# Stick-breaking scan with PSUM constants in two parts, products on POOL, a lag of four steps, and four more gate units by seven quarter products

## The chip, the cores and the metric

The kernel runs on one core of one Trainium2 chip. The metric is the device time of one execution in microseconds, the median of several runs of the same program on the same chip; lower is better. The engines are named as in the profile: PE (TensorE, matrix products; PEld is its weight load, which overlaps), DVE (VectorE), ACT (ScalarE), POOL (GpSimd) and SP (SyncE), whose queue issues nearly all DMAs.

## The reference, cut to what matters

One inference step of a hybrid encoder layer: 1024 prompt frames and 64 sample frames of 1024 channels, all in float32. Each frame is normalised and multiplied by a matrix of 1024 x 6144 columns, which gives query, key, value and gate of two attention branches with 8 heads of 64 channels each, and two branch gates of 1024 columns.

```python
# branch sb: stick breaking, s < t
z = einsum("bqhd,bkhd->bhqk", q, k) * 0.125
log_keep = where(causal, log_sigmoid(-z), 0.0)
suffix = cumsum(log_keep, axis=3, reverse=True) - log_keep
w = where(causal, exp(log_sigmoid(z) + suffix), 0.0)
o = einsum("bhqk,bkhd->bqhd", w, v)
# branch cb: softmax over the last 512 keys and the own chunk, with a clipped relative-position bias
# merge
b_sb = (o_sb * silu(z_sb)) @ w_proj_sb
b_cb = (o_cb * silu(z_cb)) @ w_proj_cb
h = sigmoid(g_sb) * b_sb + sigmoid(g_cb) * b_cb
y = x + h @ w_out
```

So a weight of branch sb is sigmoid(z) of its key times the product of sigmoid(-z) over all later keys below the query: the length of stick that is left.

## The kernel before, in words

Float32 matrices are split into a high part and a remainder, both in a format that PE multiplies at full rate, and a product is three passes (high by high, high by low, low by high). Stages, by the time in the profile:

- 0 to 227 us: normalisation, transposes, and the projections that are wanted with frames on partitions (values, queries and keys of cb).
- 227 to 483 us, line 634: twelve pairs of column units (list `pairs`: queries and keys of sb, both SiLU gates, the gate `g_sb`) by the seven-product scheme for two by two block matrices: sums of quarters of the weights are made on DVE, split on ACT and POOL, and instead of eight quarter products there are seven, each of two column pieces (256 and 288) with 4 x 3 passes. `emit` (line 563) brings the results through ACT and DVE to DRAM.
- The other eight units (list `units`, the gate `g_cb`) are plain products, line 782: each has three column groups (384, 384, 320) of 24 products. They come from a generator, `run_fill`, and are called in small numbers by `fill(n)` between the steps of the two attention stages, so that PE has work while other engines are at it; behind the units the generator goes on with the sb output projection (`proj_sb`, line 882). A group gathers in a bank of PSUM from the pool `psF`, which has two, and is copied out by ACT (`ev_act`).
- 483 to 507 us, the lead-in: six calls of `fill(24)` with the loads of the first sb pair of heads between them, all on SP: `load_k` of the sample (tile kss), `load_q` of the sample (sqs), `load_k` of the prompt (ks), `load_q` (sq), `load_v`, `load_z`.
- 507 to 680 us branch sb, 680 to 835 us branch cb. A list `seq` has, for each of four pairs of heads, the sample tile (t = 8, both heads at once) and then eight query tiles of 128 frames for either head: 17 steps. Steps of sb have 576 or (t + 1) x 128 keys, of cb 576 or up to 640.
- 835 to 985 us: projections of cb, merge and output projection.

What a step is made of, in the order of the program at iteration i: `qk(i)` has PE make the scores z (line 1033), and for sb ACT writes sigmoid(-z) into the tile kp (line 1036) and sigmoid(z) into be (line 1037), with POOL setting the one element of kp behind the last key. Then the loads for coming steps go to SP. `mid(i - 1)`, for sb, has DVE run a scan over kp from the last key to the first (line 1056): state = kp x state + constant, where the constant is a row of zeros with an identity matrix at its end (`imp`, in SBUF), which starts each row at its own query and so does the causal mask as well; then DVE multiplies be by the result (line 1057). Half of the fill follows, then `av` (line 1127: value products of a finished block of two query tiles and both heads, gated on DVE at line 1132 and stored), then `tr(i - LAG)`, which transposes the weights on PE (line 1088) into one of two PSUM tiles pt and copies them to SBUF (tile wT): for sb always on ACT (line 1097), for cb one time in four on ACT and else on DVE (line 1099). Then the other half of the fill. LAG is 3. For cb, `soft` (exponential on ACT, line 1047) and `mid` (reciprocal on DVE, scaling on ACT, line 1060) stand at the head of the iteration.

Each engine works through its own instructions in this order. Every engine's order is written out by hand; no scheduler moves anything. How many fill products an iteration gets is in proportion to its number of keys (for cb plus 150): 144 in the lead-in, 336 in sb, 288 in cb.

## Time and profile before

| | us |
|---|---|
| median of 3 runs (985.58 to 986.71) | 986.17 |
| the profiled execution | 986.78 |
| its span, first to last instruction | 985.0 |
| seven-product stage | 227 to 483 |
| lead-in | 483 to 507 |
| sb | 507 to 680 |
| cb | 680 to 835 |

The page gives the busy time of each engine and the chain of work that ended last; a busy table by stretches gives the same for each stage; the order in time of one engine shows when an instruction began and how long it took. Instructions of PE overlap, so the spacing of their starts, not their length, is what one costs. L with a number is a line of the kernel before. PE's granted clock is 1.0 throughout.

### The profile page before, as it was taken

What the parts mean: (1) busy time and instruction counts of PE and PEld (TensorE: products, weight loads), DVE (VectorE), ACT (ScalarE), POOL (GpSimd) and SP (SyncE); (2) the same over time, 40 slices, a digit from 0 to 9 for tenths busy, and PEclk for the clock granted to TensorE, in tenths of its full rate; (3) what the DMA queues carried; (4) which work ended last, traced back from release to release, by engine and by line L of the source; (5) the groups of instructions that cost most, each with busy time, mean ns of one, the idle gap of its engine ahead of it and who ended that gap; (6) DMA issues with size and microseconds to landing.
All of it is one profiled execution on the core that took longest, in us unless ns stands there. A gap on an engine that the chain in (4) does not pass through costs nothing.

```text
span 985.0 us, 20439 instructions
## 1 busy us (share of the span) xinstructions
PE 962.0 (98%) x7568; PEld 917.6 (93%) x7568; DVE 630.1 (64%) x1188; ACT 510.4 (52%) x1142; POOL 346.2 (35%) x356
## 2 busy tenths in 40 slices
PE   5999999999999999999999999999999999999998
PEld 5999999999999999999998888898888888999998
DVE  5456665696454655532239898997767765599735
ACT  5534443344443433433248787786876875466220
POOL 3376664115444554444211101101201101486641
PEclk9999999999999999999999999999999999999999
DMA  6727567533656333343298656666898772852642
GB/s 229 223 89 243 193 223 253 166 103 120 180 174 203 115 110 101 99 124 99 79 244 221 172 160 161 164 187 169 232 262 226 213 221 68 264 177 83 210 131 86
DMA packets 174243, 166.97 MB, mean 170 GB/s; under 512 B 34688, under 2 KB 160000, under 8 KB 174016
## 3 DMA queue, kind: packets, MB, share of 16 engines
q1 hardware_dynamic: 165424, 157.34, 53.7%
q10 hardware_dynamic: 8720, 8.33, 2.6%
q8 instruction: 60, 0.98, 0.4%
q14 instruction: 39, 0.32, 0.1%
HBM read 106.89 MB, written 58.72 MB: 168 GB/s over the span
## 4 chain that ended last, share of the span: by engine, by line
PE 90%; DMA 3%; ACT 3%; DVE 1%; SPq 1%; issue 1%; POOL 1%; DVEq 0%; ACTq 0%
PE b L634 25%; PE acc L464 19%; PE b L1435 8%; PE o L1127 7%; PE acc L782 7%; PE z L1033 6%; PE pt L1088 6%; PE b L924 5%; PE acc L882 3%; DMA wrawx<-in_w_in_dram 1%; PE pk L349 1%; ACT wT L1097 1%; PE pt L277 1%; SPq L51 1%; PE acc L1471 1%
## 5 line engine op out<-in xcount | busy, mean ns | idle before, releaser
L122 POOL TENSOR_TENSOR wlo<-wraw,whi 128x1024 fp32r<-128x1024 f32 x22 | 57.6, 2618 | 103.0 <-ACT whi L115 102.9
L1088 PE MATMUL pt<-ident,be 128*128 128x128 f32 (+1 forms) x568 | 87.2, 278 | 5.7 <-ACT wT L1097 1.9
L1056 DVE TENSOR_TENSOR_SCAN kp<-kp,imp 128x128 f32<-128x128 f32 (+7 forms) x64 | 88.3, 1379 | 0.6 <-ACT kp L1036 0.6
L1033 PE MATMUL z<-ks,sq 128*128 128x320 f32 (+5 forms) x384 | 83.2, 325 | 0.0
L1088 PEld LDWEIGHTS pt<-ident,be 128*128 128x128 f32 (+1 forms) x568 | 65.9, 140 | 16.8 <-issue 5.7
L1097 ACT ACTIVATE wT<-pt 128x512 f32<-128x512 f32 (+3 forms) x125 | 58.6, 501 | 39.0 <-PE pt L1088 38.9
L464 PE MATMUL acc<-whi,xa 128*128 128x256 f32 x256 | 74.2, 292 | 0.0
L464 PE MATMUL acc<-wlox,xm 128*128 128x256 f32 x256 | 70.8, 278 | 0.0
L464 PE MATMUL acc<-whi,xm 128*128 128x256 f32 x256 | 70.8, 278 | 0.0
L464 PE MATMUL acc<-wlo,xa 128*128 128x256 f32 x256 | 70.7, 278 | 0.0
L464 PE MATMUL acc<-whix,xb 128*128 128x256 f32 x256 | 70.7, 278 | 0.0
L464 PE MATMUL acc<-whix,xm 128*128 128x256 f32 x256 | 70.6, 278 | 0.0
L1033 PEld LDWEIGHTS z<-ks,sq 128*128 128x128 f32 x384 | 65.8, 188 | 1.1 <-issue 0.2
L1127 PE MATMUL o<-wT,vp 128*64 128x256 f32 (+1 forms) x608 | 66.7, 357 | 0.1
L782 PE MATMUL acc<-xm,whi 128*128 128x384 f32 (+1 forms) x192 | 65.2, 340 | 0.0
L1127 PEld LDWEIGHTS o<-wT,vp 128*64 128x64 f32 x608 | 42.3, 136 | 23.9 <-issue 5.7
L1057 DVE TENSOR_TENSOR be<-be,kp 128x128 f32<-128x128 f32 (+8 forms) x68 | 57.3, 843 | 9.4 <-ACT sg L757 0.5
L1036 ACT ACTIVATE kp<-z 128x384 f32<-128x384 f32 (+6 forms) x104 | 52.4, 504 | 9.5 <-PE z L1033 4.5
L642 DVE TENSOR_TENSOR u<-b,s 128x256 f32<-128x256 f32 (+1 forms) x48 | 20.8, 439 | 56.3 <-PE b L634 55.2
L1037 ACT ACTIVATE be<-z 128x384 f32<-128x384 f32 (+6 forms) x104 | 52.9, 508 | 0.0
L1060 ACT ACTIVATE be<-be,sm 128x640 f32<-128x640 f32 (+5 forms) x68 | 47.2, 694 | 9.5 <-DVE sm L1059 9.2
L1047 ACT ACTIVATE be<-be,sm 128x640 f32<-128x640 f32 (+5 forms) x68 | 47.2, 694 | 3.7 <-DVE sm L1039 3.4
(300 smaller groups left out, 3147.4 us busy)
## 6 DMA issues: line engine op xcount, KB each, us to landing
wraw<-in_w_in_dram SPq DMA_DIRECT2D x32, 512.0 KB, 4.6
wrawx<-in_w_in_dram SPq DMA_DIRECT2D x16, 512.0 KB, 4.5
sq<-d_qsbT SPq DMA_DIRECT2D x32, 192.0 KB, 3.6
sq<-d_qcbT SPq DMA_DIRECT2D x32, 192.0 KB, 4.4
xt<-in_x_prompt_dram SPq DMA_DIRECT2D x8, 512.0 KB, 5.8
d_kcbT<-hl SPq DMA_DIRECT2D x8, 512.0 KB, 4.4
d_qcbT<-hl SPq DMA_DIRECT2D x8, 512.0 KB, 5.7
d_ksbT<-hl SPq DMA_DIRECT2D x16, 256.0 KB, 2.5
```

Of the source, the lines that this page charges most:

```text
L122: (eng or G).tensor_tensor(out=l, in0=raw, in1=h[:].bitcast(F32), op=OP.subtract)
L464: TE.matmul(ps, x, w, start=m == 0, stop=m == len(steps) - 1)
L634: TE.matmul(ps[:, :m], w[:, hl_, k], right[s](x)[:, k, a:b], start=s < 3 and k == 0 and e == 0, stop=k == 3 and e == 2, skip_group_check=s ...
L782: TE.matmul(ps[:, :b - a], w[:, k], xk(x, k)[:, a:b], start=k == 0 and n == 0, stop=k == KT - 1 and n == 2)
L1033: TE.matmul(z[:, :m], s[:, e, q0:q0 + 128], ks[:, h, o + x:o + y], start=e == parts[0][0], stop=e == parts[-1][0])
L1037: A.activation(be[:r, x:y], z[:r, :m], AF.Sigmoid, scale=0.125)
L1056: V.tensor_tensor_scan(kp[:r, n - 1::-1], kp[:r, n - 1::-1], im[:, ::-1], 0.0, op0=OP.mult, op1=OP.add)
L1057: V.tensor_tensor(out=be[:r, :n], in0=be[:r, :n], in1=kp[:r, 1:n + 1], op=OP.mult)
L1088: TE.transpose(pt[:kr, x, :r], be[:r, kb * 128:kb * 128 + kr], ident[:r, :r])
L1097: A.activation(w[:, sl:sl + m, q0:q0 + r], pt[:, :m, :r], AF.Copy)
L1127: TE.matmul(o[hd * 64:hd * 64 + 64, c0:c1], vv[:kr, kb, hd * 64:hd * 64 + 64], wT[b, p, j, hd, s // 4][:kr, s % 4, c0:c1] if j < 4 else wT ...
L1435: TE.matmul(ps[:, t], left[s](xs_, k)[:, ts_], wt_[:, k], start=s < 3 and t == k == e == 0, stop=k == 3 and e == 2, skip_group_check=s > 2 ...
```

## The change

1. The lists: four of the eight plain units go to `pairs` as two more pairs (14 instead of 12), kind "copy".
2. The pool `psF` of two banks becomes two pools of one bank each, `psF` and `psG`, used in turn by `facc()`. During sb, `psG` holds the scan's constants (the identity, its half for the sample tile, and one zero), and fill has `psF` alone; `fill` then stops at the end of a group of 24, in the first half of an iteration one product ahead of it, and carries the rest over. In cb there are two banks again.
3. The scan is done in two parts: the last 128 keys (64 for the sample) with the identity as its constant, and the keys before them with the zero as the constant of all elements and the first part's result as its start value. The product goes from DVE to POOL.
4. LAG is 4, with one more buffer each for be and kp. In sb the copies of transposed weights alternate between ACT and DVE.
5. The lead-in has `fill(12)` six times. How much fill an iteration gets comes from a plan (`share`), which sets an estimate of PE's work in it against one of the other engines': 72 in the lead-in, 168 in sb, 228 in cb. The rest runs behind cb.
6. The last unit's first group is done in sb. Its second group, in cb, issues the loads of the sb outputs for `proj_sb`; fill is held from the end of the first group until the sixth iteration of cb.

```diff
-    units = [("ev_act", 5120 + 128 * j, (AF.Copy, d_g["cb"][j])) for j in range(KT)]
+    pairs += [("copy", 5120 + 128 * j, d_g["cb"][j:j + 2]) for j in range(0, 4, 2)]
+    units = [("ev_act", 5120 + 128 * j, (AF.Copy, d_g["cb"][j])) for j in range(4, KT)]
...
-    psF = ctx.enter_context(tc.tile_pool(name="af", bufs=2, space=PS))
+    psF = ctx.enter_context(tc.tile_pool(name="af", bufs=1, space=PS))
+    psG = ctx.enter_context(tc.tile_pool(name="ag", bufs=1, space=PS))
+    banks = [psF, psG]
+
+    def facc():
+        banks.append(banks.pop(0))
+        return banks[-1].tile([128, 512], F32, name="acc")
...
-                A.activation(sg[:, :n], src[:, :n], AF.Sigmoid)
+                A.activation(sg[:, :n], src[:, :n], AF.Copy if kind == "copy" else AF.Sigmoid)
...
-                        if ci == k == n == 0 and j + 1 == len(units):
+                        if ci == 1 and k == n == 0 and j + 1 == len(units):
                             load_og("sb", 0, late["y"])
...
-                            if ci == 2:
-                                prog[0] = j
+                            prog[0] = 3 * j + ci
...
-    def fill(n):
+    sent = [0]
+
+    def fill(n, part=2):
         n += owed[0]
         owed[0] = 0
+        room = 22 + part - sent[0] % 24 if len(banks) == 1 else n
         while n > 0:
-            if prog[0] == len(units) - 2 and "sb" not in late:
+            if room <= 0:
+                owed[0] = n
+                return
+            room -= 1
+            if prog[0] == 3 * len(units) - 3 and "sb" not in late:
...
-        be = am.tile([128, NP], F32, name="be", bufs=4)
+        be = am.tile([128, NP], F32, name="be", bufs=5)
...
-            kp = ax.tile([128, NP + 2], F32, name="kp", bufs=3)
+            kp = ax.tile([128, NP + 2], F32, name="kp", bufs=4)
...
-            im = ims[:] if t == 8 else imp[:, NP - n:NP]
-            V.tensor_tensor_scan(kp[:r, n - 1::-1], kp[:r, n - 1::-1], im[:, ::-1], 0.0, op0=OP.mult, op1=OP.add)
-            V.tensor_tensor(out=be[:r, :n], in0=be[:r, :n], in1=kp[:r, 1:n + 1], op=OP.mult)
+            m = n - (64 if t == 8 else 128)
+            imp = late["imp"]
+            last = kp[:, n - 1:m - 1 if m else None:-1]
+            V.tensor_tensor_scan(last, last, imp[:, 191:127:-1] if t == 8 else imp[:, 127::-1], 0.0,
+                                 op0=OP.mult, op1=OP.add)
+            if m:
+                V.tensor_tensor_scan(kp[:, m - 1::-1], kp[:, m - 1::-1], imp[:, 192:193].to_broadcast([128, m]),
+                                     kp[:, m:m + 1], op0=OP.mult, op1=OP.add)
+            G.tensor_tensor(out=be[:r, :n], in0=be[:r, :n], in1=kp[:r, 1:n + 1], op=OP.mult)
...
-                if b == "sb" or flip[0] % 4 == 0:
+                if flip[0] % (2 if b == "sb" else 4) == 0:
...
-        fill(24)
+        fill(12)
         flush()
         f()
+    imp = late["imp"] = psG.tile([128, 512], F32, name="acc")
+    V.tensor_copy(imp[:, 0:128], ident)
+    for h in (slice(0, 64), slice(64, 128)):
+        V.tensor_copy(imp[h, 128:192], ident[h, h])
+    V.memset(imp[:, 192:193], 0.0)
+    banks[:] = [psF]
...
-    LAG = 3
+    LAG = 4
...
+    def share(i):
+        b, p, t, hd = seq[i]
+        n = band(b, t)[1]
+        pe, v = (4 if t == 8 else 2) * n / 2.2, n * 1.45 + 900
+        if i >= LAG:
+            pe += 109 * ((band(*seq[i - LAG][::2])[1] + 127) // 128)
+        if i > LAG and closes(i - LAG - 1):
+            b2, _, t2, _ = seq[i - LAG - 1]
+            pe += sum(432 * (z - y) / 256 for _, y, z in av_steps(b2, t2 // 2 if t2 < 8 else 4))
+        if b == "sb":
+            v = 350 + (band(*seq[i - 1][::2])[1] * 2.6 if i else 0)
+        return pe, v
+
+    plan = {}
+    for b, budget in (("sb", 72 * (len(units) - 1) - 48), ("cb", 48 + FP)):
+        steps = [i for i in range(len(seq)) if seq[i][0] == b]
+        lo, hi = 0.5, 6.0
+        for _ in range(40):
+            mul = (lo + hi) / 2
+            bal, got = 0.0, []
+            for i in steps:
+                pe, v = share(i)
+                bal = max(bal + mul * v - pe, -1500)
+                got.append(max(0, int(bal / 165)))
+                bal -= 165 * got[-1]
+            if sum(got) <= budget:
+                lo, best = mul, got
+            else:
+                hi = mul
+        plan.update(zip(steps, best))
+        plan[steps[-1]] += budget - sum(best)
...
-            acc += amount[b] * wt[b](band(b, t)[1]) / tot[b]
-            if (b, p, t) == ("cb", 0, 8):
-                acc += 12
-            m = int(acc) - emitted
-            emitted += m
+            m = plan[i]
...
-        if i < len(seq) and seq[i][:3] == ("cb", 0, 1) and hd == 1:
+        if i == len(seq) // 2 + 1:
+            banks[:] = [psG, psF]
+        if i == len(seq) // 2 + LAG + 1:
             late["sb"] = True
-        fill(m // 2)
+        fill(m // 2, 1)
```

47 lines of the change are left out of this document (20 added, 27 removed).

## The prediction

> **What bounds the kernel now.** I read the page first, then the busy table cut at the stage borders, then the chain, then the order in time of single engines where the diff works.
>
> ```profile
> span 985.0 us, 20439 instructions
> PE 962.0 (98%) x7568; PEld 917.6 (93%) x7568; DVE 630.1 (64%) x1188; ACT 510.4 (52%) x1142; POOL 346.2 (35%) x356
> ```
> ```profile
> 227.00:483.00 256.00, 256.00 (x2062) 255.13 (x2061) 119.53 (x233) 99.94 (x229) 121.45 (x84) 1.00 0.43 129
> 483.00:507.00 24.00, 24.00 (x149) 24.00 (x148) 1.91 (x4) 4.78 (x9) 6.82 (x8) 1.00 0.71 194
> 507.00:680.00 173.00, 170.05 (x1259) 149.28 (x1257) 155.43 (x164) 136.18 (x333) 22.22 (x74) 1.00 0.69 185
> 680.00:835.00 155.00, 151.52 (x1168) 131.05 (x1169) 105.33 (x388) 112.76 (x255) 17.00 (x22) 1.00 0.70 195
> ```
> Columns: stretch, its length, then busy time of PE, PEld, DVE, ACT and POOL, the clock, DMA. PE is busy everywhere: in the seven-product stage (227 to 483), in the lead-in (483 to 507), in the stick-breaking stage "sb" (507 to 680) and in the band stage "cb" (680 to 835). In sb DVE is close behind, 155 of 173. So PE work is the currency, and the question is whether PE stays the only bound once work is taken from it.
>
> **Seven products for four more gate units.**
>
> ```profile
> 301.28 181.86 PE b L634 x1464
> ...
> 483.14 4.17 PE acc L782 x24
> ```
> ```profile
> 503.20 0.31 PE L782 MATMUL acc<-xa,whi 128*128 128x320 f32 x1
> ...
> 506.57 0.31 PE L782 MATMUL acc<-xm,wlo 128*128 128x320 f32 x1
> ```
> A product of the quarter scheme takes 181.86/1464 = 0.1242 us. Two pairs of units are 2 x 7 x 24 = 336 of them: +41.7 us in a stage where PE is never idle, so all of it counts. A plain product takes 4.17/24 = 0.174 us at 384 columns and (506.57 - 503.20)/23 = 0.147 at 320; a unit is 48 of the first and 24 of the second, 11.85 us, mean 0.165. Four units are -47.4 us. The sums, splits, evictions and weight loads of two more pairs are a sixth of what the stage does already beside PE (DVE 120, ACT 100, POOL 121 of 256): nothing. So PE has 5.7 us less to do in all. But the 47.4 us leave stages where those products fill PE while other engines work, and they count only where PE was what the stage waited for. By the fill counts in the two programs, the lead-in loses 72 of 144, sb 168 of 336, cb 60 of 288, of which 12 (of the sb projection) merely run later.
>
> **Lead-in.**
>
> ```profile
> 485.15 2.43 SPq L51 DMA_DIRECT2D kss<-d_csbT  x4
> ...
> 490.86 2.48 SPq L51 DMA_DIRECT2D sqs<-d_qsbT  x4
> ...
> 495.65 2.39 SPq L51 DMA_DIRECT2D ks<-d_ksbT  x4
> ...
> 499.19 2.48 SPq L51 DMA_DIRECT2D sq<-d_qsbT  x4
> ```
> ```profile
> 506.71 1.22 PE L1033 MATMUL z<-kss,sqs 128*128 128x288 f32 x8
> ...
> 508.47 0.33 PE L1033 MATMUL z<-ks,sq 128*128 128x128 f32 x2
> ```
> Each issue holds SP for about 0.62 us, and what stands ahead of the first prompt scores (8 kss, 4 sqs, 4 ks, 4 sq, a weight load, a store) is some 22 issues from 2.15 us after the stage's start at 483.0: they end near 16.2 us. In before they end at 501.67, 18.7 us. Landing takes 2 to 5 us (the issue at 499.19 to the use at 508.47 bounds it by 9.3), say 3.4: the data are there at 19.6 us. PE, with 72 products (11.9 us) and the sample tile's scores (1.1), is free at 13 and idles 6.5. Before, these scores came 25.5 us after 483.0. So -6 us, not -11.9 (bounds -4 and -9).
>
> **Scan in two parts, product on POOL.**
>
> ```profile
> L1056 DVE TENSOR_TENSOR_SCAN kp<-kp,imp 128x1024 f32<-128x1024 f32 x8 | 18.2, 2281 | 0.0
> ...
> L1056 DVE TENSOR_TENSOR_SCAN kp<-kp,imp 128x128 f32<-128x128 f32 x8 | 3.3, 417 | 0.0
> ```
> ```profile
> L1057 DVE TENSOR_TENSOR be<-be,kp 128x128 f32<-128x128 f32 (+8 forms) x68 | 57.3, 843 | 9.4 <-ACT sg L757 0.5
> L642 DVE TENSOR_TENSOR u<-b,s 128x256 f32<-128x256 f32 (+1 forms) x48 | 20.8, 439 | 56.3 <-PE b L634 55.2 <-ACT s L638 0.8
> L1099 DVE COPY wT<-pt 128x384 f32<-128x384 f32 (+3 forms) x75 | 35.8, 494 | 6.3 <-PE pt L1088 5.8
> L1097 ACT ACTIVATE wT<-pt 128x512 f32<-128x512 f32 (+3 forms) x125 | 58.6, 501 | 39.0 <-PE pt L1088 38.9
> ```
> ```profile
> 519.15 0.69 DVE L1057 TENSOR_TENSOR be<-be,kp 128x512 f32<-128x512 f32 x1
> ...
> 521.44 2.61 DVE L1057 TENSOR_TENSOR be<-be,kp 128x512 f32<-128x512 f32 x1
> ...
> 675.33 2.29 DVE L1056 TENSOR_TENSOR_SCAN kp<-kp,imp 128x1024 f32<-128x1024 f32 x1
> 677.75 1.23 DVE L1057 TENSOR_TENSOR be<-be,kp 128x1024 f32<-128x1024 f32 x1
> ```
> ```profile
> 520.86 2.64 POOL L122 TENSOR_TENSOR wlo<-wraw,whi 128x1024 fp32r<-128x1024 f32 x1 [4.38 <-ACT whi L115]
> ...
> 707.43 1.98 POOL L848 TENSOR_TENSOR xb<-ot,xa 128x384 fp32r<-128x384 f32 x2
> ```
> The scan costs (2281 - 417)/896 = 2.08 ns an element and 0.15 us each time. Constants in PSUM are not shown by any scan here; the nearest row with one PSUM input is L642, 439 ns at a mean of 272 elements, no dearer than a product from SBUF. I take no surcharge; a bound is 0.06 us for each of 124 scans, none below nothing. The second part waits for the first: 677.75 - 675.33 - 2.29 = 0.13 us. DVE loses 57.3 us of products, and gains 60 second starts (0.15 + 0.13, 17 us) and half of sb's 100 copies of transposed weights (50 x 0.49, 25 us); ACT is relieved of those 25. POOL does a 384-element product in 0.99 us, 1024 in 2.4 to 2.6: some 100 us over the stage, hidden beside a scan of 2.4 us, and the fourth step of lag covers its longer way to the transposes.
>
> Why PSUM: at 521.44 a DVE product of two SBUF operands took 2.61 us instead of 0.69 and ended with POOL's L122 (520.86 + 2.64). The Trainium skill (SBUF — State Buffer, "Who interferes with whom") says that a Vector instruction with two SBUF inputs and a GpSimd one that reads SBUF block each other, and with one SBUF input not; the trace agrees with the first half, and no run here shows the second. A rule speaks against the change: the Trainium skill (Perfetto Trace Analysis, "Optimizing Scalar/DVE Operations") gives Vector about 65 ns more overhead with PSUM than with SBUF, an estimate of 8 us more over 124 scans, and a sum some 5 us higher where DVE leads; L642 does not bear it out.
>
> **What sb then takes.**
>
> ```profile
> 527.04 1.73 PE L1127 MATMUL o<-wT,vp 128*64 128x256 f32 x16
> 528.71 0.77 PE L1088 MATMUL pt<-ident,be 128*128 128x128 f32 x5
> ...
> 677.71 0.33 PE L1033 MATMUL z<-ks,sq 128*128 128x128 f32 x2
> ...
> 678.08 1.03 PE L1088 MATMUL pt<-ident,be 128*128 128x128 f32 x8
> 678.87 0.39 PE L782 MATMUL acc<-xm,wlo 128*128 128x320 f32 x1
> ...
> 707.85 0.74 PE L1033 MATMUL z<-ks,sq 128*128 128x320 f32 x4
> 708.43 0.34 PE L782 MATMUL acc<-xb,whi 128*128 128x384 f32 x1
> ...
> 709.77 0.74 PE L1033 MATMUL z<-ks,sq 128*128 128x320 f32 x4
> ```
> From the first prompt scores to cb's, 508.47 to 677.71, are 169.2 us, four rounds of 17 steps. Were PE the only bound, 168 products less are -27.7. But DVE now also carries copies that wait for PE's transposes of the same step, behind that step's scan; so it can no longer run ahead while PE does a long row of value products, and PE cannot run more than about a step ahead of DVE. I therefore set both beside each other step by step. PE: scores 0.58 us per 1280 columns, a transpose 0.79/8 = 0.099, value products 1.67/16 = 0.104 each, 0.12 per step for changes between them, plus the plan's fill (at most 8 products, none in 10 of 17 steps of a steady round, counted from the program) at 0.165. DVE: the scan of the step before, half the copies, the gating. For a steady round, PE/DVE from the sample tile on: 4.4/3.4, 0.9/2.0, 1.0/1.0, 1.2/1.0, 4.2/1.5, 1.5/1.1, 0.6/1.2, 0.8/1.2, 1.5/1.5, 1.8/2.0, 2.0/1.8, 2.1/1.9, 2.2/2.2, 3.1/2.7, 2.0/2.6, 2.5/2.6, 3.0/2.9. The sums are 34.7 and 32.6; the larger of each step add up to 37.8. The first round has no values of a previous one and 57 instead of 37 fills: 32 to 34. Lockstep gives 3 x 37.8 + 34 and some 3 for changes that the steps don't show, 150 us; PE alone 169.2 - 27.7 = 141.5. With about a step of slack I take the middle, 145: -24 us, bounds -28 and -18 (the PSUM surcharge put in where DVE leads). PE would stand idle here for some 4 us, for transposes whose buffers DVE has not emptied, where now it hardly waits.
>
> One bank for the fill instead of two: the program stops fill at the end of a group of 24, so its eviction (about 0.5 us on ACT) lies behind scores and values; seven groups, at most 0.5 us each, inside those bounds.
>
> **cb and the end.** A step of 640 keys takes 709.77 - 707.85 = 1.92 us with five products in it, full on PE. 48 products fewer are -7.9; the plan also keeps them out of steps with value products. But steps that ACT and DVE hold near 1.9 us gain nothing from it: -6 (bounds -11 and -2). The last unit's second group now issues the loads of the sb outputs and has the first conversion right behind them on ACT:
>
> ```profile
> 712.61 3.12 DMA ot<-d_osb
> ```
> That wait of some 3 us stands ahead of the exponentials; the lag hides part: +2 (0 to 4). The 12 products pushed past cb fill a place where PE waits for DMAs anyway: 0 (up to +2).
>
> **Sum** against the profiled execution's own 986.78 us (span 985.0 and 1.8 around it, 0.6 above the median of 986.17): +41.7 - 6 - 24 - 6 + 2 = +7.7, 994.5; less the 0.6 for a median, 994.
>
> **Rivals.** (1) Faster: the copies on DVE do not tie it to PE, since they alternate with ACT's and two transpose buffers give enough slack; then sb is PE's alone and cb gains fully: 41.7 - 7 - 27.7 - 9 + 0 = -2, and with the plan's better placing up to -6: 981 to 984. For it: DVE's sum is under PE's over a round (32.6 to 34.7). Against it: seven of 17 steps have DVE ahead, most of them in runs. It decides if a steady round takes under 36 us. (2) No change: sb near 143 us and cb -7, so that the lead-in's idle 6 us just eats PE's 5.7: 985 to 988. (3) Much slower: the scan's start value, read from SBUF, or its one SBUF operand does block POOL, and scan and product run one after the other, as at 521.44. POOL's 24 us a round (2.2 ns by 9792 elements and starts) added to DVE's 32.6 is 57 a round, 226 us for sb: 986 + 41.7 - 6 + 57 - 6, about 1073. Only a lock decides it.
>
> **Chances.** Forecast 0.60; (1) 0.20; (2) 0.14; (3) 0.06. A measurement tells 0.2% (2 us) from no change. Faster 0.21, same 0.14, slower 0.65. The forecast's own range is 989 to 1004 (sb from -28 to -18 and the rest within half of their bounds, as they will not all fall together); rivals (1) and (2) take its lower end to 981.
>
> **What would show it.** The seven-product stage 41.7 us longer, at 0.124 us a product; PE idle about 6 us between unit products and the first prompt scores; scans of 2.08 ns an element, unchanged beside a running POOL product; steady rounds of 36.5 to 38 us instead of 42.3, with PE's transposes waiting for DVE copies; POOL near 110 us in sb. Wrong: rounds at 35 us or less, scans stretched to the product's end, or first scores within 14 us of the stage's start.

## The result, and the profile after

The changed kernel takes 1021.29 us, median of four runs (1019.0 to 1022.2), beside 986.44 us for the kernel before on the same chip (985.58 to 989.44): 1.0344 times, 95% interval 1.0315 to 1.0373. It is slower, as forecast, but by 35 us and not by 8; 994 was forecast, with a range up to 1004. The profiled execution took 1022.05 us, with a span of 1020.1.

The busy table, cut at the borders that the prediction used (first unit product after the seven-product stage, first prompt scores of sb, first prompt scores of cb, first product of the next projection). First the kernel before, then the changed one. The columns are as in the prediction: stretch, length, busy time of PE, PEld, DVE, ACT and POOL, granted clock, DMA share, GB/s.

```profile
482.98:508.47 25.49, 25.49 (x159) 25.49 (x158) 1.91 (x4) 6.21 (x13) 6.82 (x8) 1.00 0.74 199
508.47:677.71 169.24, 166.65 (x1233) 146.12 (x1233) 153.60 (x158) 132.48 (x325) 22.22 (x74) 1.00 0.69 184
677.71:849.30 171.59, 166.43 (x1263) 145.47 (x1262) 113.32 (x402) 120.03 (x267) 24.08 (x27) 1.00 0.70 198
849.30:985.00 135.70, 131.90 (x1026) 131.53 (x1024) 95.31 (x119) 51.83 (x81) 70.55 (x42) 1.00 0.48 153
```
```profile
227.00:523.26 296.26, 296.26 (x2385) 295.39 (x2384) 133.30 (x260) 114.24 (x261) 138.23 (x99) 1.00 0.41 126
523.26:546.64 23.38, 13.05 (x82) 12.85 (x81) 2.83 (x7) 4.13 (x9) 3.70 (x5) 0.86 0.67 160
546.64:697.34 150.70, 142.97 (x1046) 118.81 (x1046) 126.84 (x194) 106.18 (x263) 86.35 (x137) 0.99 0.71 188
697.34:885.38 188.04, 170.11 (x1238) 146.26 (x1237) 116.39 (x407) 120.73 (x267) 25.70 (x28) 0.96 0.65 184
885.38:1020.00 134.62, 130.97 (x1026) 130.77 (x1024) 94.02 (x119) 50.29 (x80) 70.79 (x42) 1.00 0.47 149
```

| stretch | before | after | difference | forecast |
|---|---|---|---|---|
| up to the end of the seven-product stage | 482.98 | 523.26 | +40.3 | +41.7 |
| lead-in, to the first prompt scores of sb | 25.49 | 23.38 | -2.1 | -6 (-9 to -4) |
| sb, to the first prompt scores of cb | 169.24 | 150.70 | -18.5 | -24 (-28 to -18) |
| cb and the rest of the sb projection | 171.59 | 188.04 | +16.5 | -6 and +2 (at most +4) |
| the end | 135.7 | 134.6 | -1.1 | 0 |

The differences add up to 35.1 of the 35.3 us between the two profiled executions. The first row is the forecast. The lead-in gave 3.9 us less than expected and sb 5.5. The fourth row has the wrong sign and is 20 us off: more than half of the miss lies in a stage whose scores, exponentials and value products the change leaves as they were. PE has 25 instructions fewer in it and works 3.7 us longer; its clock is 0.96 there and was 1.00; and it stands still for 18 us instead of 5.

What PE waited for in cb, from the view of waits (engine, line, what it waited for: total, times, longest):

```profile
PE z L1039 <- DMA sqs<-d_qcbT: 4.9, 1, 4.9
PE pt L1100 <- DVE wT L1111: 3.7, 7, 0.8
PE acc L881 <- DVE xm L885: 2.2, 1, 2.2
PE o L1134 <- DVE wT L1111: 1.9, 4, 1.0
```

The largest is a transfer that is late, so the next thing to read is the queue that issues it (PE's waits in the kernel before are 4.4 us in seven, none of them for a transfer). SP's waits for the gate tile `zt` (line 1105 before, 1117 after) are these, before and after:

```profile
SPq L1105 <- DMA d_ocb<-zt: 4.0, 3, 1.4
```
```profile
SPq L1117 <- DMA d_ocb<-zt: 16.5, 7, 3.8
```

And the queue in order of time, with the row of PE that waited at its end:

```profile
792.92 1.00 SPq L695 DMA_DIRECT2D d_ocb<-zt  x2
797.58 0.32 SPq L1117 DMA_DIRECT2D zt<-d_zcb  x1
...
808.81 5.05 SPq L51 DMA_DIRECT2D sqs<-d_qcbT  x4
...
815.22 2.26 PE L1039 MATMUL z<-kss,sqs 128*128 128x288 f32 x8 [4.95 <-DMA sqs<-d_qcbT]
817.40 3.54 PE L1134 MATMUL o<-wT,vp 128*64 128x256 f32 x24
```

The two stores of output tiles end on SP at 793.92, and the load of the next gate tile is issued at 797.58. Gate and output share the tile: a value block is multiplied into its `zt` in place, stored from there, and only then may the next gate be loaded into it. With three such tiles and four steps of lag the load needs the tile whose store has just been issued, and SP, which works in order, stands for 3.7 us until that store has landed. Everything behind it is late: the queries `sqs` of the next round are issued from 808.81 on and PE waits 4.95 us for them. Their own four issues take 5.05 us, of which SP stands 2.4 for a load of weights (`wraw`), so not all of the delay is the tile's. Then PE runs slower still, at a granted clock of 0.50 for 3.4 us: eight score products take 2.26 us (1.21 or 1.22 in the kernel before), 24 value products 3.54 (2.38 to 2.41 at six of the seven places in its cb).

### The profile page after: what moved, and what is told of

Its sections match the earlier page's. It is cut to its first block, busy times and chain, and to the rows that moved or that the text cites. A ratio compares the mean times of both kernels' runs of the same rounds, so it can differ in the third digit from the quotient of the medians.

```text
span 1020.1 us, 20722 instructions
## 1 busy us (share of the span) xinstructions
PE 970.0 (95%) x7616; PEld 919.0 (90%) x7616; DVE 620.3 (61%) x1259; ACT 496.8 (49%) x1110; POOL 426.7 (42%) x432
## 4 chain that ended last, share of the span: by engine, by line
PE 84%; DMA 4%; ACT 4%; SPq 3%; DVE 2%; issue 1%; POOL 0%; ACTq 0%; POOLq 0%; DVEq 0%
PE b L642 29%; PE acc L472 19%; PE b L1485 7%; PE o L1134 7%; PE pt L1100 5%; PE b L923 5%; PE z L1039 4%; PE acc L881 4%; PE acc L782 2%; SPq L51 2%; DMA wraw<-in_w_proj_sb_dram 1%; ACT wT L1109 1%; DVE wT L1111 1%; ACT be L1043 1%; PE pk L357 1%
## 5 line engine op out<-in xcount | busy, mean ns | idle before, releaser
L1069 POOL TENSOR_TENSOR be<-be,kp 128x128 f32<-128x128 f32 (+8 forms) x68 | 82.0, 1206 | 77.3 <-DVE kp L1067 41.3
L1039 PE MATMUL z<-ks,sq 128*128 128x320 f32 (+5 forms) x384 | 88.8, 340 | 13.4 <-DMA d_gcb<-sg 10.3
L122 POOL TENSOR_TENSOR wlo<-wraw,whi 128x1024 fp32r<-128x1024 f32 x18 | 43.6, 2422 | 95.5 <-ACT whi L115 95.3
L1067 DVE TENSOR_TENSOR_SCAN kp<-kp,acc 128x512 f32<-128x512 f32 (+6 forms) x60 | 76.8, 1280 | 2.1
L1134 PE MATMUL o<-wT,vp 128*64 128x256 f32 (+1 forms) x608 | 71.5, 365 | 1.5 <-DVE wT L1111 1.2
L1111 DVE COPY wT<-pt 128x512 f32<-128x512 f32 (+3 forms) x125 | 63.2, 517 | 12.2 <-PE pt L1100 11.4
L1134 PEld LDWEIGHTS o<-wT,vp 128*64 128x64 f32 x608 | 45.9, 140 | 25.5 <-issue 6.1
L1109 ACT ACTIVATE wT<-pt 128x512 f32<-128x512 f32 (+3 forms) x75 | 36.7, 489 | 49.0 <-PE pt L1100 48.8
L442 POOL TENSOR_TENSOR whix<-ws,whix 128x512 fp32r<-128x512 f32 x28 | 37.0, 1320 | 41.9 <-ACT whix L441 41.9
L1072 ACT ACTIVATE be<-be,sm 128x640 f32<-128x640 f32 (+5 forms) x68 | 47.1, 693 | 11.4 <-DVE sm L1071 11.3
```

The costliest lines, as they stand in the source:

```text
L1039: TE.matmul(z[:, :m], s[:, e, q0:q0 + 128], ks[:, h, o + x:o + y], start=e == parts[0][0], stop=e == parts[-1][0])
L1067: V.tensor_tensor_scan(kp[:, m - 1::-1], kp[:, m - 1::-1], imp[:, 192:193].to_broadcast([128, m]), kp[:, m:m + 1], op0=OP.mult, op1=OP.add)
L1069: G.tensor_tensor(out=be[:r, :n], in0=be[:r, :n], in1=kp[:r, 1:n + 1], op=OP.mult)
L1111: V.tensor_copy(w[:, sl:sl + m, q0:q0 + r], pt[:, :m, :r])
L1134: TE.matmul(o[hd * 64:hd * 64 + 64, c0:c1], vv[:kr, kb, hd * 64:hd * 64 + 64], wT[b, p, j, hd, s // 4][:kr, s % 4, c0:c1] if j < 4 else wT ...
```

## The experiments

**The gate tiles (theory A).** Each ratio below is to the kernel before on the same chip. One edit, five tiles instead of three:

```diff
-        zt = am.tile([128, 256], F32, name="zt", bufs=3)
+        zt = am.tile([128, 256], F32, name="zt", bufs=5)
```

> The changed kernel with five gate buffers zt instead of three. Theory A (the lag makes each zt tile live a step longer, so the load of the next one waits in SP's queue for a store that has just been issued, every load behind it is late, and PE stops and then runs at a lower clock): SP's waits for d_ocb<-zt, 16.5 us in seven, fall to 0 to 3 us; the stretch from the cb sample scores to the end of the sb projection falls from 192.8 to 177 to 185 us, and the time from 1021.3 to 1004 to 1014 us. Theory B (the loads are late for another reason: SP's queue is full, or the fill stands in the wrong steps): the waits on zt go but the stretch stays within 3 us of 192.8 and the time within 3 us of 1021.

Measured: 1012.71 us, 1.0252 times the kernel before (1.0236 to 1.0267), which took 988.15 us on that chip; the changed kernel's ratio is 1.0344, 0.9% above. SP's wait on line 1117 is gone. The same place in the queue (SP):

```profile
786.75 1.78 SPq L695 DMA_DIRECT2D d_ocb<-zt  x2
788.59 0.47 SPq L1117 DMA_DIRECT2D zt<-d_zcb  x1
...
799.11 3.76 SPq L51 DMA_DIRECT2D sqs<-d_qcbT  x4
...
808.51 1.21 PE L1039 MATMUL z<-kss,sqs 128*128 128x288 f32 x8
```
```profile
698.56:875.25 176.69, 164.78 (x1239) 142.71 (x1238) 116.35 (x407) 118.90 (x266) 26.04 (x28) 1.00 0.69 193
```

The load now follows the stores at once, the queries are there when PE comes, the clock is 1.00, and cb is 11.4 us shorter (188.04 to 176.69 by the prediction's border, 192.8 to 181.4 by the expectation's, which begins at the cb sample scores). Theory A holds, for about 11 of the 16.5 us.

**A lag of three, without and with the five tiles.**

```diff
-    LAG = 4
+    LAG = 3
```

> The changed kernel with a lag of three steps instead of four; nothing else. Theory A: the zt tiles are given back a step earlier, so cb falls from 192.8 to 178 to 186 us; sb, where the product on POOL stands in the way to the transposes, becomes 1 to 6 us longer than its 145.9; in all 1008 to 1018 us. Theory B: cb stays within 3 us of 192.8 and the time is 1020 to 1028 us, as only sb changes.

> The changed kernel with five zt buffers and a lag of three steps. If the fourth step of lag costs cb what its border shows (one more row of 24 value products and a group of transposes in it, 3.9 us, and a longer drain), cb falls from the 181.4 us of five buffers alone to 175 to 179. With the lag of three alone (three zt buffers) cb took 184.2 us, and its first round 49.5, in which PE stood 2.4 and 2.8 us behind conversions that waited for their loads; SP's 2 us or so of waits for zt were no part of that. If those conversions are tied to the lag, the first round stays at 47 to 50 us here too, cb at 182 to 186, and the time at 1016 to 1020 us; without them 1008 to 1013 us.

Measured: 1018.71 us, 1.0315 times (1.0299 to 1.0331), with three tiles; 1021.41, 1.0317 (1.0293 to 1.0341), with five. With this lag the number of tiles changes nothing (SP's wait on line 1117 is 4.7 us in four with three tiles, 4.0 in the kernel before), so the long wait for `zt` belongs to the fourth step. The time is nearly that of the changed kernel nevertheless. sb is 3 to 4 us longer (153.9 and 154.7). The first cb round takes 49.5 and 50.6 us, where five tiles and a lag of four give 42.8. PE runs as many instructions in it, to within four, so this is waiting. ACT shows where much of it comes from, in the run with five tiles:

```profile
730.01 0.52 ACT L842 ACTIVATE xa<-ot 128x384 fp32r<-128x384 f32 x1 [3.33 <-DMA ot<-d_osb]
734.45 0.52 ACT L842 ACTIVATE xa<-ot 128x384 fp32r<-128x384 f32 x1 [2.49 <-DMA ot<-d_osb]
```

Two conversions of sb outputs wait for their loads, ahead of exponentials, and PE waits 1.90 and 2.54 us behind them; its clock is 0.87 over the round. With a lag of four these waits of PE are 1.20 and 0.96 us and the clock stays at 1.00. The other three rounds and the rest of the projection tell what the fourth step moves there; three rows, from the kernel with five tiles and a lag of four, from that with five and three, and from the kernel before:

```profile
736.58:875.25 138.67, 130.77 (x990) 114.75 (x990) 92.43 (x322) 89.98 (x202) 17.05 (x18) 1.00 0.68 190
```
```profile
750.99:885.76 134.77, 126.51 (x960) 113.52 (x959) 90.41 (x317) 87.74 (x194) 15.96 (x17) 1.00 0.68 189
```
```profile
714.26:849.30 135.04, 130.50 (x984) 114.28 (x983) 90.32 (x318) 90.81 (x201) 18.15 (x19) 1.00 0.71 200
```

The fourth step moves the last step's transposes and value products across a border: 30 PE instructions and 3.9 us more lie behind the start of the second round. That is work which before lay in front of it. Over the whole kernel the fourth step pays once its tiles are there: with five tiles the ratio is 1.0252 with it and 1.0317 without. Of the expectation for the lag of three with five tiles the second half came true (its 1016 to 1020 was a little low); with three tiles cb fell, by the expectation's border, from 192.8 to 184.2 us as theory A had it, and the time was 0.7 us above its range.

**The fill's places in cb (theory B).** In proportion to the keys, as before, instead of by the plan:

```diff
+    steps = [i for i in range(len(seq)) if seq[i][0] == "cb"]
+    even, done = 0.0, 0
+    for i in steps:
+        even += (48 + FP) * (band(*seq[i][::2])[1] + 150) / sum(band(*seq[k][::2])[1] + 150 for k in steps)
+        plan[i] = int(even + 1e-6) - done
+        done += plan[i]
```

> The changed kernel with its 228 cb fill products dealt out in proportion to the keys of a step plus 150, as the kernel before does it, instead of by the plan; nothing else. Theory B, in the form that the plan puts the fill where PE is not short of work and leaves the steps empty in which it waits: cb falls by 5 to 12 us, the time to 1009 to 1016 us. Theory A: the loads are as late as before, the fill covers some of the waits by chance only: within 4 us of 1021.

Measured: 1018.71 us, 1.032 times (1.0295 to 1.0346): within 4 us, as theory A said. SP's wait on line 1117 is 17.6 us in seven, and PE waits 8.2 us in two for `sqs`. The fill's places are not the cause.

**The conversions of the sb outputs.** First kept back for 12 products, then given earlier loads, both with five tiles:

```diff
+        late["wait"] = late.get("wait", 0) - 1
-        if ogq and now:
+        if ogq and now and late["wait"] <= 0:
...
                             load_og("sb", 0, late["y"])
+                            late["wait"] = 12
```
```diff
                             load_og("sb", 0, late["y"])
+                            load_og("sb", 1, late["y"])
...
-                ots[ci, p] = stage.tile([128, 384], F32, name="ot", bufs=4)
+                ots[ci, p] = stage.tile([128, 384], F32, name="ot", bufs=8)
...
-            if f is og_hi and p and ci < 2:
-                load_og("sb", ci + 1, late["y"], [p - 1])
+            if f is og_hi and p and ci < 1:
+                load_og("sb", ci + 2, late["y"], [p - 1])
...
```

> The changed kernel with five zt buffers (1012.7 us), and the first conversion of the sb outputs on ACT kept back for 12 fill products after the loads that it waits for. If those waits (5.3 us of ACT in three, ahead of exponentials) hold PE up in the first cb round, as the prediction's +2 says, that round falls from 42.8 us by 1 to 3 us, PE's two waits of 1.2 and 0.96 us at 725 to 728 go, and the time is 1009.5 to 1011.5 us. If the lag hides them, the time is within 1 us of 1012.7. A load that is late for a conversion in the projection would cost 1 us or more instead.

> The changed kernel with five zt buffers (1012.7 us), and eight instead of four buffers for the sb outputs that ACT converts, the first two column groups loaded at once where the first alone was loaded before; the first conversion still stands right behind its load. If those waits hold PE up, ACT's later ones (5.3 us in three, the longest 3.0) go but for the first of about 1 us, PE's waits of 1.2 and 0.96 us at 725 to 728 go with them, the first cb round falls from 42.8 us to 40 to 42, the time to 1009 to 1011.5 us. If the four loads more ahead of SP's other loads cost as much, or the lag hides the waits, it is within 1 us of 1012.7.

Kept back: 1015.39 us, 1.0272 times (1.0233 to 1.031), no gain. ACT's waits for these loads grow from 5.3 to 8.3 us, the first round stays at 42.9, and in the second PE waits 3.06 us behind one (40.5 us instead of 36.1). With earlier loads ACT waits 1.1 us in one, PE's two waits go, and the first round falls from 42.8 to 40.0 as expected; but in the second PE waits for queries that the four additional loads have put back on SP, and it takes 38.8 instead of 36.1. From PE in that run:

```profile
732.76 1.03 PE L1040 MATMUL z<-kss,sqs 128*128 128x288 f32 x6 [0.40 <-DMA sqs<-d_qcbT]
...
739.27 0.41 PE L1040 MATMUL z<-ks,sq 128*128 128x128 f32 x2 [0.91 <-DMA sq<-d_qcbT]
```

1011.49 us, 1.0243 (1.0209 to 1.0277), no difference from five tiles alone that the intervals show. The conversions do cost the first round 2.8 us; in this run, loads that come earlier on SP made others late.

**The two halves apart.** The scan part alone: the pairs and the fill counts undone, with five tiles (lag, copies and the plan for the fill stay as changed). The pairs alone: put into the kernel before.

```diff
-    pairs += [("copy", 5120 + 128 * j, d_g["cb"][j:j + 2]) for j in range(0, 4, 2)]
-    units = [("ev_act", 5120 + 128 * j, (AF.Copy, d_g["cb"][j])) for j in range(4, KT)]
+    units = [("ev_act", 5120 + 128 * j, (AF.Copy, d_g["cb"][j])) for j in range(KT)]
...
-        fill(12)
+        fill(24)
...
-    for b, budget in (("sb", 72 * (len(units) - 1) - 48), ("cb", 48 + FP)):
+    for b, budget in (("sb", 72 * (len(units) - 2) - 108), ("cb", 108 + FP)):
```
```diff
+    pairs += [("copy", 5120 + 128 * j, d_g["cb"][j:j + 2]) for j in range(0, 4, 2)]
-    units = [("ev_act", 5120 + 128 * j, (AF.Copy, d_g["cb"][j])) for j in range(KT)]
+    units = [("ev_act", 5120 + 128 * j, (AF.Copy, d_g["cb"][j])) for j in range(4, KT)]
...
-        fill(24)
+        fill(12)
...
-    n_sb = 72 * 5 - 24
-    n_cb = 72 * (len(units) - 2) - n_sb + FP
+    n_sb = 72 * 2 - 24
+    n_cb = 72 * (len(units) - 1) - n_sb + FP
```

> The scan part of the change alone: the changed kernel with five zt buffers, but the eight gate units of cb all as plain three-term products again, 144 in the lead-in, 324 in sb and 288 in cb, as the kernel before has them to within 12. The seven-product stage ends 40 us earlier than in the changed kernel, at 483. sb then has the PE work of before (169 us from prompt scores to prompt scores, of which PE idled 3), DVE about 30 us less: if PE bounds it, 160 to 169 us. cb has 3.9 us more from the lag at its border and else what before has: 176 to 182. Time 980 to 992 us; so the scan part alone is worth little either way. The other theory, that the longer lag and the copies cost PE more than the scan saves: 993 us or more.

> The other part alone: the kernel before, with the two further pairs of gate units in the seven-product stage, 72 instead of 144 products in the lead-in, 120 instead of 336 in sb and 276 instead of 288 in cb; scan, products, lag and copies as before. The stage ends 40 to 42 us later. If sb is then bound by DVE, which has 155 us of work in it whatever PE does, it falls from 169 to 157 to 163 us only, and the time is 1013 to 1022 us. If PE bounds it still, 216 products of 0.165 go, 35 us: 988 to 994 us.

Measured, beside 989.04 us before on that chip: the scan part 1000.35, 1.0105 times (1.008 to 1.0129); the pairs 1030.0, 1.0405 times (1.0376 to 1.0435). sb in the one and the other:

```profile
507.04:676.74 169.70, 164.86 (x1203) 141.12 (x1202) 130.49 (x197) 114.12 (x276) 94.46 (x142) 1.00 0.70 184
```
```profile
546.35:715.13 168.78, 151.43 (x1019) 120.67 (x1020) 143.25 (x154) 124.99 (x312) 12.33 (x70) 0.92 0.65 166
```

This is the clearest pair of the study. sb took 169.24 us before. With 23 us less for DVE it takes 169.70; with some 214 PE instructions less it takes 168.78; with both it takes 150.70. Taking work from either engine alone gave nothing. In the first of the two PE is busy 164.86 us, so PE holds the stage. In the second neither engine is full, PE busy 151.43 us at a granted clock of 0.92 and DVE 143.25, and the rounds stay at 42 to 44 us (43 before); which waits between the two hold them there was not taken apart. The pairs without the scan part lose the whole 40 us of their products, and my expectation (157 to 163, DVE's busy time plus a little) missed that DVE's 143 us of work were spread over 169.

For the scan part alone sb is as expected if PE bounds it (160 to 169), but the time is that of the other theory (993 or more): it loses in cb, 187.06 us there against 171.59, though with five tiles. The extra step at the border, later conversions and a wait of 3.9 us in the projection are seen in it, and its parts were not taken away one by one.

**What the scan part rests on.** The constants in an SBUF tile, and the product on DVE again:

```diff
-    imp = late["imp"] = psG.tile([128, 512], F32, name="acc")
+    imp = late["imp"] = ax.tile([128, 200], F32, name="imp", bufs=1)
```
```diff
-            G.tensor_tensor(out=be[:r, :n], in0=be[:r, :n], in1=kp[:r, 1:n + 1], op=OP.mult)
+            V.tensor_tensor(out=be[:r, :n], in0=be[:r, :n], in1=kp[:r, 1:n + 1], op=OP.mult)
```

> The changed kernel with the scan's constants (the 193 columns that the two-part scan reads) in an SBUF tile instead of the PSUM bank; the bank stays reserved and unused. If a scan with two SBUF operands and a POOL product block each other, a scan of 1024 elements beside a product is stretched from 2.3 us to 3.5 us or more and sb, 145.9 us, becomes 190 to 230 us: 1065 to 1105 us. If they do not, the scans stay at 2.08 ns an element and the time within 3 us of 1021.

> The changed kernel with the product with the stick lengths on DVE again; the two-part scan, the PSUM constants, the copies and the lag as changed. DVE then has 57 us more in sb, 33 + 14 us a round with 2 to 5 us of waits: rounds of 46 to 52 us instead of 38.4, sb 30 to 50 us longer, the time 1050 to 1070 us, if DVE is what the stage waits for next to PE. If the chain through POOL (scan, product on POOL, transpose) set the rounds, the shorter way would take back part of it: 1021 to 1045 us.

Constants in SBUF: 1069.44 us, 1.0821 times (1.0801 to 1.0841), sb 198.67 us. DVE and POOL there, and DVE and POOL of the changed kernel with the constants in PSUM:

```profile
676.48 1.49 DVE L1064 TENSOR_TENSOR_SCAN kp<-kp,imp 128x128 f32<-128x128 f32 x1
...
683.97 3.15 DVE L1067 TENSOR_TENSOR_SCAN kp<-kp,imp 128x768 f32<-128x768 f32 x1
...
676.15 1.55 POOL L1069 TENSOR_TENSOR be<-be,kp 128x768 f32<-128x768 f32 x1 [1.48 <-DVE kp L1067]
...
683.59 1.91 POOL L1069 TENSOR_TENSOR be<-be,kp 128x896 f32<-128x896 f32 x1 [2.27 <-DVE kp L1067]
```
```profile
649.08 0.41 DVE L1064 TENSOR_TENSOR_SCAN kp<-kp,acc 128x128 f32<-128x128 f32 x1
649.52 1.81 DVE L1067 TENSOR_TENSOR_SCAN kp<-kp,acc 128x768 f32<-128x768 f32 x1
...
649.15 1.78 POOL L1069 TENSOR_TENSOR be<-be,kp 128x896 f32<-128x896 f32 x1 [1.99 <-DVE kp L1067]
```

Where a product runs, a 128-column scan takes 1.49 instead of 0.41 and ends within 0.3 us of the product, and a 768-column one 3.15 instead of 1.81. From PSUM both keep their time. A lock as in rival (3) exists, then, but with two SBUF operands and not with one: it costs 48 us of sb, and the bank in PSUM is what avoids it. The Trainium skill (SBUF — State Buffer, "Who interferes with whom") calls the port that DVE's second SBUF operand shares with POOL an exclusive lock; both halves of the rule are now shown here, 3.15 us with two SBUF operands and 1.81 with one.

Product on DVE: 1076.35 us, 1.0888 times (1.0857 to 1.0918), sb 202.08 us with DVE busy 176.74 of them, rounds of 51 to 53. The expectation had the rounds nearly right (46 to 52), its time was 6 us low. Moving the product to POOL was worth 51 us of sb, and without it the rest of the scan part would have made DVE the bound.

**What holds a steady sb round.** The prediction tied DVE and PE by the copies of transposed weights that it gave to DVE. Four runs test it: all copies on ACT; 72 products moved from sb to the lead-in (with five tiles); the same with the gating behind the next step's scan (or ahead of the next value block, where that comes first); and with both ties cut.

```diff
-                if flip[0] % (2 if b == "sb" else 4) == 0:
+                if b == "sb" or flip[0] % 4 == 0:
```
```diff
-        fill(12)
+        fill(24)
...
-    for b, budget in (("sb", 72 * (len(units) - 1) - 48), ("cb", 48 + FP)):
+    for b, budget in (("sb", 72 * (len(units) - 2) - 48), ("cb", 48 + FP)):
```
```diff
-        V.tensor_tensor(out=os[:, :nq], in0=o[:, :nq], in1=os[:, :nq], op=OP.mult)
-        store_later(d_o[b][p][:, 256 * j:256 * j + nq], os[:, :nq])
+        def gate():
+            V.tensor_tensor(out=os[:, :nq], in0=o[:, :nq], in1=os[:, :nq], op=OP.mult)
+            store_later(d_o[b][p][:, 256 * j:256 * j + nq], os[:, :nq])
+
+        gateq.append(gate)
...
             mid(i - 1)
+        gates()
         flush()
```

> The changed kernel with all copies of the transposed weights in the stick-breaking stage on ACT again, as before; nothing else. Theory L (lockstep: the copies tie DVE to PE, and a round takes the larger of the two step by step): without them DVE has 25 us less to do and can run ahead, a steady round goes from 38.4 us (mean of 37.1, 40.0, 38.0) to 35 to 37, the time from 1021.3 to 1010 to 1017 us. The other theory (the copies cost nothing on DVE, and ACT's copies come late instead, behind its exponentials): the rounds stay within 1 us or grow, the time is 1020 to 1028 us.

> The changed kernel with five zt buffers, and 24 instead of 12 products at each of the six places in the lead-in, 72 products that the sb stage then has less (96 instead of 168). Compared with the five buffers alone (1012.7 us). Theory L: PE's idle 10 us of the lead-in take up the 72 products, the first prompt scores stay within 3 us of 23.2 us after the stage's start, and the products after them no longer run at half speed; sb, where these products count only in the steps in which PE is behind DVE, falls by 5 to 9 us from 147.1: 1003 to 1008 us. If PE alone bounds sb: 72 products of 0.165, 12 us less, 998 to 1002 us. If DVE alone does: within 2 us of 1012.7.

> The kernel of the 24-product lead-in (five zt buffers, 24 products a place in the lead-in, 96 in sb; 1012.8 us), with the gating product of a value block put behind the next step's scan on DVE instead of ahead of it. In that kernel a steady sb round takes 36.9 to 39.1 us though PE has 18 products less in it than in the changed kernel. Theory G: DVE, in order, stands 10.7 us in three rounds at a gating whose value products are still running, with a scan that could run behind it; without that the rounds become 34 to 36.5 us, sb 6 to 12 us shorter (147.7 from prompt scores to prompt scores), the time 1001 to 1008 us. Theory C: that idle time lies where no scan is ready anyway, since the scores behind the value products are not there, and the round is held by the chain scores, exponential, scan, product, transpose over four steps: rounds within 0.7 us, the time within 3 us of 1012.8.

> The kernel of the 24-product lead-in (five zt buffers; 1012.8 us) with both of DVE's ties to PE taken away in sb: the gating behind the next step's scan, and all copies of the transposed weights on ACT. If DVE stands still because its next instruction in order, whichever it is, waits for PE's value products, then scans can now run on behind them: steady rounds fall from 36.9 to 39.1 us to 33.5 to 36.5, sb from 147.7 to 137 to 144 us, the time to 1003 to 1010 us (if ACT, which then has the 25 us of copies, does not become the tie). If the tie is on the other side, PE's transposes waiting for two buffers that either engine empties late, or the chain over four steps, the rounds stay within 1 us and the time is 1010 to 1022 us.

| run | steady rounds | sb | time | ratio (95%) |
|---|---|---|---|---|
| changed kernel | 37.1, 40.0, 38.0 | 150.70 | 1021.29 | 1.0344 (1.0315 to 1.0373) |
| copies on ACT | 37.8, 39.8, 38.1 | 152.43 | 1024.89 | 1.035 (1.0323 to 1.0377) |
| five tiles | 37.1, 40.0, 38.0 | 151.85 | 1012.71 | 1.0252 (1.0236 to 1.0267) |
| and 72 products in the lead-in | 36.9, 37.6, 39.1 | 147.67 | 1012.80 | 1.0232 (1.0204 to 1.026) |
| and the gating later | 37.3, 39.0, 39.3 | 149.93 | 1019.45 | 1.0313 (1.0289 to 1.0338) |
| and the copies on ACT | 36.7, 36.5, 38.6 | 146.73 | 1020.48 | 1.0311 (1.0284 to 1.0338) |

A steady round is counted from one sample tile's scores to the next, over the second to the fourth of sb. Its mean is 38.4, 38.6, 38.4, 37.9, 38.5 and 37.3 us down the table: no edit takes more than 1.1 us from it. With 54 products less in three rounds, 8.9 us at 0.165, they are 1.5 us shorter. The waits of DVE show how each edit moves the wait instead of taking it away; the view of waits over three rounds, for 72 products in the lead-in, for the gating later, and for both ties cut:

```profile
DVE zt L1139 <- PE o L1134: 10.7, 8, 2.7
DVE wT L1111 <- PE pt L1100: 3.9, 10, 0.6
```
```profile
DVE wT L1111 <- PE pt L1100: 14.4, 13, 3.3
DVE zt L1147 <- PE o L1141: 2.6, 2, 1.3
```
```profile
DVE kp L1064 <- ACT kp L1042: 21.7, 34, 1.4
DVE zt L1147 <- PE o L1141: 6.4, 4, 1.8
```

First DVE stands at the gating, then at the copy behind the same value products, and without either at ACT's sigmoid of the scores (kp), which PE issues behind those products. So the copies are not the tie, and theory L in the form of the prediction falls; so does theory G. What holds the rounds near 37 us looks by these waits like a chain through PE, ACT and DVE, in which PE is busy 103.61 of 111.75 us (both ties cut, rounds two to four), ACT 91.59 and DVE 80.97. Which link sets it was not separated, and stays open. The later gating also makes cb longer (184.3 us, and 187.7 with both ties cut, against 178.4), which is why these two runs are no faster. The 72 products moved took 4.2 us from sb where theory L had 5 to 9, and the time stayed where it was; the gating later has the rounds of theory C and not its time.

**The lead-in** is shown by the run with 72 products in it. The stretch from the stage's end to the first prompt scores, with 144 products, and the first 3.4 us after it with 72 (changed kernel):

```profile
523.60:548.39 24.79, 24.79 (x155) 24.79 (x153) 1.26 (x5) 5.51 (x11) 4.85 (x4) 1.00 0.70 184
```
```profile
546.64:550.00 3.36, 3.35 (x12) 3.36 (x13) 0.74 (x2) 0.89 (x4) 0.45 (x2) 0.50 1.02 284
```

Twice the products cost 1.6 us more than in the kernel with five tiles (23.2). The 72 products that the change took out of the lead-in thus gained almost nothing there, and in sb they now cost 4.2 of the 11.9 us that PE needs for them.

No run came below the kernel before. By the PE work alone the change could have gained 5.7 us at most.

## Why the prediction was wrong

**Seven products: right.** 336 more of them, 40.3 us. The chain has the stage as one row, 223.61/1800 = 0.1242 us a product:

```profile
299.83 223.61 PE b L642 x1800
```

336 of that are 41.7; the row begins 1.4 us earlier than before.

**Lead-in: right sign, a third of the size.** The issues were right, the landing was not. From SP and PE:

```profile
537.34 2.75 SPq L51 DMA_DIRECT2D sq<-d_qsbT  x4
...
546.64 0.66 PE L1039 MATMUL z<-ks,sq 128*128 128x128 f32 x2 [10.33 <-DMA d_gcb<-sg]
```

The last issue ends at 540.09, 16.8 us after the stage's end (16.2 forecast), but the scores start 6.5 us later and not 3.4. The bound that I had quoted, 9.3 us from issue to use, allowed this. (The row names a store that landed at about the same time; PE's weight load for the same scores waited 10.54 us for `sq`, and with five tiles the product's own row names `sq`.) PE idles 10.3 us and not 6.5, and then runs at a clock of 0.50 for 3.4 us, a price that no term of the sum had.

**sb: -18.5, at the edge of its bounds.** The prediction had two values, 150 for lockstep and 141.5 for PE alone, and took the middle, 145, "with about a step of slack". The measured 150.7 is lockstep without slack, and its table (37.8 a steady round) gives the rounds: 37.1, 40.0, 38.0. The step that failed is the slack. The reason given for the lockstep, the copies on DVE, is not borne out either: with the copies on ACT the rounds are the same. That the size fits is in part luck: the table has PE at work 34.7 us in a round and idle 3.1, and over the three rounds PE was busy 108.61 of 115.19 us, 36.2 a round, and idle 2.2.

**Scan and product: right.** No scan is stretched by the product. By form, the kernel before first and then the changed one:

```profile
L1056 DVE TENSOR_TENSOR_SCAN kp<-kp,imp 128x896 f32<-128x896 f32 x8 | 16.1, 2017 | 0.0
```
```profile
L1064 DVE TENSOR_TENSOR_SCAN kp<-kp,acc 128x128 f32<-128x128 f32 x64 | 26.1, 408 | 11.6 <-ACT kp L1042 11.5
L1067 DVE TENSOR_TENSOR_SCAN kp<-kp,acc 128x896 f32<-128x896 f32 x8 | 16.6, 2080 | 0.3
L1069 POOL TENSOR_TENSOR be<-be,kp 128x1024 f32<-128x1024 f32 x8 | 16.0, 1998 | 9.0 <-DVE kp L1067 3.9 <-ACT be L1043 3.1 <-DMA sq<-d_qcbT 2.1
```

The surcharge for PSUM was rightly taken as nothing (408 ns for 128 columns, 417 before); the rule of the Trainium skill quoted against it does not show here. The second part does take 63 ns more than a scan of as many columns before (2080 and 2017), but PSUM is not the reason: with the constants in SBUF, second parts that no product disturbs take the same 2.08 us. They differ from the scan before in the start value from a tile and the one zero used for all elements; which of these costs the 63 ns was not tried. Two terms were taken too dear without effect: the second part starts 0.03 us after the first (649.08 + 0.41 to 649.52), not 0.13, and a 1024-column product takes 2.00 us on POOL, not 2.4, so POOL is busy 86.35 us in sb and not near 110.

**cb: the step that failed.** "But steps that ACT and DVE hold near 1.9 us gain nothing from it: -6 (bounds -11 and -2)" priced only the 48 products that leave. The fourth step of lag was costed once, as cover for POOL in sb, and never as what it is for every other buffer: one step more of life. be and kp got a tile more each in the diff; `zt`, which the diff does not touch, did not, and its three tiles were not set beside the new lag. Five tiles give back 11.4 us of cb's 16.5; this much is shown by taking the cause away. Of the remaining 5.1, the lag's step at the border is 3.9, work moved across it, in a stretch that gains only 0.3 us from its fewer products (134.77 us with the lag of three, 135.04 before), where -6 had been forecast for all of cb. The waits of conversions, forecast at +2 (0 to 4), cost the first round 2.8 in the kernel with five tiles, by the run with earlier loads. These two and what the first round saved were not separated further.

**The rivals.** (1) and (2) needed an sb near 143 us or less and did not happen. (3) did not happen either: one SBUF operand and the start value do not block POOL. With the constants in SBUF, two operands, the lock is there, but that 1069.44 us were measured and 1073 worked out is luck. The working had 226 us for sb and -6 for cb; sb took 198.67, and cb 187.1, 15.5 more than before.

Two figures of the working do not follow from it: by its own terms the range begins at 985 (994 - 4 - 1.5 - 2.5 - 1) and not at 989, and DVE is ahead in six of the table's 17 steps, not seven. Neither bears on the miss.

## What to carry to other kernels

A longer pipeline lengthens the life of every tile that crosses it, not only of those that the change touches: count the buffers of each, and ask what stands behind a load that waits for one in an in-order queue. When two engines are nearly equally busy in a stage (here PE 166.65 and DVE 153.60 of 169.24 us), taking work from one alone may give nothing, as it did here; do both in one experiment and each alone. A long wait in front of PE was paid twice here: 4.95 us as idle time, and again at a clock of 0.50 for 3.4 us after it.

## What the runs showed of the hardware

After standing still, PE ran at half speed for a time in these runs. After 10.33 us of idle the granted clock was 0.50 for the next 3.4 us; after 4.95 us it was so too, and eight products took 2.26 instead of 1.21. The Trainium skill (TensorE: Matmul & The Clock Gate, "What's actually happening") gives an idle window of about 3.4 us for the drop and as much for the return; the 3.4 us until the return agree. But shorter waits also did it when two came close together, in the kernel with a lag of three:

```profile
728.40 0.66 PE L1100 MATMUL pt<-ident,be 128*128 128x128 f32 x4 [2.38 <-ACT be L1072]
...
732.77 0.90 PE L1039 MATMUL z<-ks,sq 128*128 128x320 f32 x2 [2.83 <-DVE sm L1045]
733.60 3.72 PE L1134 MATMUL o<-wT,vp 128*64 128x256 f32 x16
```

Sixteen value products take 3.72 us there and 1.73 to 1.75 elsewhere in that run; the granted clock is 0.50 from 732.77 to 737.40. A wait of 2.73 us by itself, in the kernel with five tiles, was followed by products at full speed (0.31 us each at 320 columns, as before).
